# Where the second rows are turned in the first projection, and when two of its sums are made

## The chip, the cores and the metric

The kernel runs on one core of a Trainium2 chip. A core has TensorE (PE, matmuls from SBUF into PSUM), VectorE (DVE), ScalarE (ACT), GpSimd (POOL) and the DMA queues, of which SyncE (SP) issues most here. The engines run side by side, each through its own list of instructions, and wait for one another by semaphores. The metric is the device time of one execution in microseconds (us); several executions give a median.

## The reference, cut to what matters

One layer over 2048 rows of 1024 columns, all in float32: x_n = RMSNorm(x); an input projection z = x_n W_in; a pooling branch and a gated linear recurrence (HGRN2) on parts of z; sigmoid gates; an output projection; a gated feed-forward part; a last RMSNorm.

```python
xn = rmsnorm(x, norm1_g[l])
z = xn @ w_in[l]
u_pool, zq, zf, zi, zo, zg = jnp.split(z, splits, axis=-1)
```

The change touches the part of z that the kernel computes first: the columns of zi and zo (v and z in the kernel), 1024 columns in all, for the first 1024 rows.

## The kernel before, in words

**Blocks.** Rows are handled 1024 at a time (two halves of 512: `b0` and `b0 + 1`, "first rows" and "second rows"), so everything happens twice. A multiplication of the two row halves by the two halves of the weights is done in the seven-product way of Strassen and Winograd: seven passes P1 to P7 instead of eight. Each pass multiplies one form of the activations by one form of the weights.

**Forms.** `FORM` (line 52) names the activation form of each pass. B11 and B21 are the two column halves of the first rows, turned (transposed on TensorE by `transpose`, line 675, so that the columns lie on the partitions) and scaled by the norm's gain. B12 and B22 are the same of the second rows (B22 carried with a minus sign). The sums are T1 = B12 - B11, T2 = B22 - T1 (both by `minus`, line 762, straight from PSUM), T3 = B12 - B22 and T4 = B21 - T2. Each form has four tiles of 128 x 512, numbered 0 to 3. They are written T20 to T23, T30 to T33 and so on in the trace; x_t<-x_t,cols,... rows of L765 are the sums themselves.

**High and low halves.** A float32 product is made of three matmuls with operands cut to a shorter format. `split` (line 608) makes the two halves of a form: ScalarE casts the high half (x_T20h), then VectorE subtracts it from the whole and has the low half (x_T20l). The weights are cut the same way in `Stream.convert` (line 198): cast on ScalarE (L211), low half on VectorE (L212), into one of six operand tiles (`ops`), which come free when TensorE is done with them. A sum, its cast on ScalarE and its low half on VectorE are thus a round trip between two engines.

**The first projection**, `proj_io` (line 1166), runs the passes in the order of `IO_ORDER`: P1, P2, P6, P5, P7, P4, P3, which I call the first to the seventh pass. In each of them four weight tiles (k) are multiplied with four groups of 128 rows (j), each j with a PSUM bank of its own: 48 matmuls of 128 x 512 a pass. P1 goes into four banks called X, P2 into four Y, P6, P7 and P4 into the same four Z, P5 and P3 into four V. There are eight banks in all. `after` (line 1185) evacuates: after P6 it makes u2 = e1 - Z (L1191), after P7 u3 = Z - e1 (L1193), after P4 z from Z. Since P4 starts its banks Z anew, its first matmul follows u3. After P2 `out_v` (line 1174) makes v = e1 + Y and stores it from SP's queue.

**Weights of the passes.** P1, P2 and P4 take stored quarters of the weights. P6, P7 and P3 take sums of quarters, made in `plan_io`'s function `fn` (line 347, L351 on VectorE) when the tile's turn comes: two sums for each of P6's four tiles (w8 to w11 in the trace, for T20 to T23), one for P7's and P3's. Sums that are used again are stored to DRAM by `keep` and read back, among them P5's weights, which are P6's first sums.

**The second rows** are prepared by `forms_b_task` (line 746). When `go_io` is set, it does for k = 0 to 3: two banks of transpositions (`turned`), B22 on ScalarE, T1 and T2 on VectorE, T3 on VectorE, then the split of T2. After this loop come the splits of T1, of T3, then T4 and B22. The task is stepped once in so many matmuls (`mm`, line 145), or when a pass needs its form.

**What sets the order.** The kernel's text gives an order of issue, and a scheduler with a time model of its own then orders each engine's list when the program is built, by what depends on what. `behind(ins, other)` (line 239) binds an instruction to come after another on its engine, without a wait.

Of the kernel before, what the change touches and what calls it, by code (L numbers as in the profile page):

```python
# [15 lines left out]
ALU = mybir.AluOpType  # L16
# [36 lines left out]
FIRST = ("P1", "P6", "P5")  # L53
# [26 lines left out]
def tile_trunk(  # L80
# [26 lines left out]
    def slot(name, cols=TB, dt=F32):  # L107
        return slots.tile([P, cols], dt, tag="s", name=name, padded_shape=[P, 528])
# [4 lines left out]
    def f32(ap):  # L113
        return ap.bitcast(F32)
# [43 lines left out]
    class Stream:  # L158
# [39 lines left out]
        def convert(self):  # L198
            j = len(self.tiles)
            key, fn, raws = self.ops[j]  # L200
            while any(r.tile is None for r in raws):
                self.load()
            store_kept()
            v = fn(f"w{j}")
            t = opsp.tile([P, 2, 512], F32R, tag="ops", name=f"ops{j}")
            n = int(np.prod(v.shape[1:]))
            hi, lo = t[:, 0, :n], t[:, 1, :n]
            if len(v.shape) == 3:
                hi = hi.rearrange("p (a b) -> p a b", a=v.shape[1])
                lo = lo.rearrange("p (a b) -> p a b", a=v.shape[1])  # L210
            self.mark = act.copy(hi, v)  # L211
            low = dve.tensor_tensor(lo, v, f32(hi), ALU.subtract)  # L212
            if j in self.pins:
                for ins, other in zip((self.mark, low), self.pins[j]):
                    behind(ins, other)
            self.tiles.append((key, t))
            self.load_ahead()
# [21 lines left out]
    def behind(ins, other):  # L239

        tc.add_manual_dep(ins.ins, other.ins.name, mybir.DependencyInfo(
            mybir.DependencyClass.NoSync, mybir.DependencyReason.DATA), reason="behind")
# [17 lines left out]
    stream = Stream()  # L260
# [347 lines left out]
    def split(src, name, on_pool=False):  # L608
        hi = slot(name + "h", TB, F32R)
        lo = slot(name + "l", TB, F32R)  # L610
        if on_pool:
            pool.tensor_scalar(hi, src, 1.0, 0.0, ALU.mult, ALU.add)
        else:
            act.copy(hi, src)
        dve.tensor_tensor(lo, src, f32(hi), ALU.subtract)
        return hi, lo
# [10 lines left out]
    def n_step(ps, w, xk, j, first, last, mark=None, **kw):  # L627
        xh, xl = xk
        a, b = xh[:, j * P : (j + 1) * P], xl[:, j * P : (j + 1) * P]
        mm(ps, a, w[:, 0], start=first, stop=False, **kw)  # L630
        if mark is not None:
            behind(count[1], mark)
        mm(ps, a, w[:, 1], start=False, stop=False, **kw)
        mm(ps, b, w[:, 0], start=False, stop=last, **kw)
# [40 lines left out]
    def transpose(ps, xs, j, k):  # L675
        c = (k % 4) * P
        return pe.transpose(ps[:, j * P : (j + 1) * P], xs[j, k // 4][:, c : c + P], ident)
# [68 lines left out]
    def forms_b_task(src, gain, forms, full, after, go, early):  # L746
        name = f"{src[0]}{src[1]}_"
        xs = {}
        while early and not forms["B21"]:
            yield 1  # L750
        yield from norm_rows(src, name, xs, after, int(early))
        while not go():
            yield 2
        t1, b12, b22 = [], [], []

        def turned(k):
            ps = bank(f"{name}t{k}")
            for j in range(NT):
                transpose(ps, xs, j, k)
            return ps  # L760

        def minus(key, k, ps, x1, c=None, op=ALU.subtract):
            t = slot(f"{name}{key}{k}")
            c = gain + (k if c is None else c)
            dve.scalar_tensor_tensor(t, ps, col(c), x1, ALU.mult, op)  # L765
            return t


        t3 = []
        for k in range(4):  # L770
            while len(full["B11"]) <= k:
                yield 4
            p12 = turned(k)
            p22 = turned(k + 4)
            t = slot(f"{name}b{k}")
            act.activation(t, p22, AF.Copy, scale=negs[:, gain + k + 4 : gain + k + 5])
            b22.append(t)
            t1.append(minus("t1", k, p12, full["B11"][k]))
            t2 = minus("t2", k, p22, t1[k], k + 4)
            if src[0] == "m":  # L780
                t = slot(f"{name}t3{k}")
                pool.tensor_tensor(t, full["B11"][k], t2, ALU.subtract)
                t3.append(t)
            else:
                t3.append(minus("t3", k, p12, b22[k], op=ALU.add))
            forms["T2"].append(split(t2, f"{name}T2{k}"))
            full["T2"].append(t2)
            yield 1
        for k in range(4):
            forms["T1"].append(split(t1[k], f"{name}T1{k}"))  # L790
            yield 5
        for k in range(4):
            forms["T3"].append(split(t3[k], f"{name}T3{k}"))
            yield 1
        for k in range(4):
            while len(full["B21"]) <= k:
                yield 4
            t4 = slot(f"{name}t4{k}")
            (dve if src[0] == "x" else pool).tensor_tensor(t4, full["B21"][k], full["T2"][k],
                                                           ALU.subtract)  # L800
            forms["T4"].append(split(t4, f"{name}T4{k}"))
            forms["B22"].append(split(b22[k], f"{name}B22{k}"))
            yield 1
# [231 lines left out]
    def value(dst, a, ps):  # L1035
        if a is None:
            act.copy(dst, ps)
            return
        t, how = a
        if how == "from":  # L1040
            dve.tensor_tensor(dst, ps, t, ALU.subtract)  # L1041
        else:
            dve.tensor_tensor(dst, t, ps, ALU.add if how == "add" else ALU.subtract)  # L1043

    class Unit:
        def __init__(self, name, key, emit):
# [119 lines left out]
    def proj_io(b0, forms, late, vd, zd):  # L1166
        bk = {}
        e1, u2, u3 = {}, {}, {}

        def temp(d, key, j):  # L1170
            d[j] = slot(f"io{b0}_{key}_{j}")
            return d[j]

        def out_v(hf, j, a):
            t = slot(f"v{b0}_{hf}_{j}")
            value(t, a, bk["Y" if hf == 0 else "V"][j])
            sp.dma_start(vd[hf][:, j, :], t)

        def out_z(hf, j, a):
            t = slot(f"z{b0}_{hf}_{j}")  # L1180
            value(t, a, bk["Z" if hf == 0 else "V"][j])
            act.activation(t, t, AF.Silu)
            sp.dma_start(zd[hf][:, j, :], t)

        def after(p, j):
            if p == "P1":
                act.copy(temp(e1, "e1", j), bk["X"][j])
            elif p == "P2":
                out_v(0, j, (e1[j], "add"))
            elif p == "P6":  # L1190
                dve.tensor_tensor(temp(u2, "u2", j), e1[j], bk["Z"][j], ALU.subtract)  # L1191
            elif p == "P7":
                dve.tensor_tensor(temp(u3, "u3", j), bk["Z"][j], e1[j], ALU.subtract)  # L1193
                out_z(1, j, (u3[j], "add"))
            elif p == "P4":
                out_z(0, j, (e1[j], "from"))
            elif p == "P3":
                out_v(1, j, (u2[j], "sub"))

        for p in IO_ORDER:  # L1200
            if p == "P7" and not b0:
                setup.append(Task(setup_task()))
            xs = need(forms, FORM[p], late)
            kb = "Y" if p == "P2" else BANK[p]
            if kb not in bk:
                bk[kb] = [bank(f"io{b0}_{kb}_{j}") for j in range(NT)]
            for k in range(4):
                if (p, k) == GO_IO[b0 > 0]:
                    go_io[0] = True
                w = stream.get("io")  # L1210
                if (p, k, b0) == ("P1", 0, 0):
                    xh, xl = xs[0]
                    for n in range(3):
                        for j in range(NT):
                            mm(bk[kb][j], (xl if n == 2 else xh)[:, j * P : (j + 1) * P],
                               w[:, n % 2], start=n == 0, stop=False, skip_group_check=True)
                    stream.used(1)
                    continue
                for j in range(NT):
                    n_step(bk[kb][j], w, xs[k], j, p in FIRST + ("P2",) and k == 0, k == 3,  # L1220
                           skip_group_check=True)
                    if k == 3:
                        after(p, j)
                stream.used(1)
# [453 lines left out]
    for b in range(0, SEQ // TB, 2):  # L1678
        forms, task, late = nxt
# [55 lines left out]
```

## Time and profile before

| | us |
|---|---|
| median of 3 runs | 2563.47 |
| the three runs | 2560.06, 2567.12, 2563.47 |
| the profiled execution | 2558.88 |
| its span | 2557.1 |
| mean granted clock of TensorE in it | 0.996 |

The span runs from the first to the last instruction of the profiled execution; its time holds 1.8 us more around it. Rows of a timeline read: start, duration, engine, line, operation, tile written <- tiles read, shapes, and in brackets the idle time before it with the engine or DMA that ended it. A duration runs to the end of the last write, so two rows in sequence may overlap a little, and the pitch from start to start is what an instruction occupies. Tables of stretches give the busy time of each engine, then the granted clock (1.00 is full), the share of the DMA engines and GB/s. Line numbers are those of the kernel before; in the changed kernel, lines from 785 on stand some lines further down.

### The profile page before, as it was taken

Reading aid. Unit: us, or ns where it says so; the run is one execution under the profiler, and the core shown is the slowest. Engines: PE = TensorE matmul, PEld = TensorE weight load, DVE = VectorE, ACT = ScalarE, POOL = GpSimd, SP = SyncE. Lnnn points to the kernel's source line nnn. Section 1 sums busy time; section 2 is a strip of 40 time slices with the busy share of each in tenths; the row PEclk is TensorE's granted clock in tenths of the full one; section 3 lists DMA queues with packets and bytes.
Section 4 is the critical chain, followed back from the end, with each engine's and each line's share of the span. In section 5 each row is a group of like instructions: output and inputs, shape, how many; then the busy total and the mean of one; then the engine's idle time right before and its main releaser. Section 6 shows DMA issues by size and latency. Waiting matters only on the chain.

```text
span 2557.1 us, 35636 instructions
## 1 busy us (share of the span) xinstructions
PE 2518.8 (99%) x11508; PEld 2057.1 (80%) x11508; DVE 1980.0 (77%) x3518; ACT 1176.9 (46%) x2218; POOL 759.2 (30%) x1117
## 2 busy tenths in 40 slices
PE   8999999999999999999999999999999999999998
PEld 7787887888788888888887888888887888888887
DVE  7798778588899787885585877775978987778755
ACT  6433434324545454554454343442355554545534
POOL 1444344002544334461230111200034433325410
PEclk9999999999999999999999999999999999999999
DMA  7778758768788879997344343446442444446952
GB/s 249 246 195 220 211 179 243 235 209 245 193 244 245 222 227 240 258 356 257 131 153 149 98 137 111 129 155 224 147 162 95 155 150 144 147 138 230 332 163 99
DMA packets 252332, 493.76 MB, mean 193 GB/s; under 512 B 26544, under 2 KB 43056, under 8 KB 251824
## 3 DMA queue, kind: packets, MB, share of 16 engines
q1 hardware_dynamic: 185664, 315.70, 38.3%
q0 software_dynamic: 41504, 110.64, 16.8%
q10 hardware_dynamic: 24976, 65.13, 7.4%
q8 instruction: 91, 1.49, 0.2%
q14 instruction: 97, 0.79, 0.1%
HBM read 381.79 MB, written 187.17 MB: 222 GB/s over the span
## 4 chain that ended last, share of the span: by engine, by line
PE 92%; DVE 4%; issue 1%; DMA 1%; ACT 1%; POOL 0%; SPq 0%; ACTq 0%; DVEq 0%; POOLq 0%
PE dn_P L146 16%; PE up_Z L146 14%; PE up_X L146 10%; PE up_V L146 9%; PE wo_P L146 6%; PE gr_Z L146 4%; PE pb L146 3%; PE pa L146 3%; PE gr_X L146 3%; PE gr_V L146 3%; PE io_Z L146 2%; PE fr_Z L146 2%; PE io_V L146 2%; PE fr_X L146 2%; PE fr_V L146 2%; PE pl L918 1%
## 5 line engine op out<-in xcount | busy, mean ns | idle before, releaser
L211 ACT CAST ops<-raw 128x512 fp32r<-128x512 f32 x736 | 454.4, 620 | 844.4 <-PE dn_P L146 179.5
L212 DVE TENSOR_TENSOR ops<-raw,ops 128x512 fp32r<-128x512 f32 x736 | 547.5, 747 | 201.3 <-ACT ops L211 192.8
L1471 DVE SCALAR_TENSOR_TENSOR e<-h,cols,e 128x512 f32<-128x512 f32 x176 | 143.6, 818 | 31.2 <-ACT e L1469 24.1
L1469 ACT ACTIVATE e<-h,cols 128x512 f32<-128x512 f32 x176 | 142.5, 814 | 24.9 <-DVE h L1043 18.5
L1474 DVE SCALAR_TENSOR_TENSOR e<-h,cols,e 128x512 f32<-128x512 f32 x176 | 133.9, 769 | 2.8
L861 POOL DMA_DIRECT2D g_P<-dg_P x154 | 84.4, 555 | 162.4 <-PE dn_P L146 111.1
L1150 POOL TENSOR_TENSOR gf_P<-e,e 128x512 f32<-128x512 f32 x44 | 61.2, 1392 | 149.3 <-DVE e L1480 95.8
L1266 POOL TENSOR_TENSOR q<-q,qs 128x512 f32<-128x512 f32 x16 | 21.9, 1368 | 198.3 <-ACT qs L1265 150.8
L1150 POOL TENSOR_TENSOR gf_P<-gf_P,e 128x512 f32<-128x512 f32 x44 | 59.2, 1344 | 72.1 <-DVE e L1480 71.7
L1464 POOL COPY h<-h 128x2 f32<-128x2 f32 x88 | 40.2, 468 | 114.3 <-DVE h L1041 107.5
L1478 ACT ACTIVATE e<-e 128x512 f32<-128x512 f32 x88 | 55.6, 632 | 38.4 <-DVE e L1474 38.2
L1466 POOL COPY hist<-h 128x2 f32<-128x2 f32 x88 | 35.8, 407 | 118.7 <-DVE h L1043 116.9
L1043 DVE TENSOR_TENSOR h<-up_u,up_V 128x512 f32<-128x512 f32 x88 | 60.1, 683 | 13.4 <-PE up_V L146 12.9
L1303 ACT ACTIVATE gt<-gt,cols 128x512 f32<-128x512 f32 x48 | 34.8, 725 | 75.1 <-DVE gt L1043 61.0
L1125 DVE TENSOR_TENSOR x<-x,wo_P 128x512 f32<-128x512 f32 x88 | 56.1, 683 | 12.1 <-PE wo_P L146 11.9
L910 POOL COPY qm<-q 128x64 f32<-128x64 f32 x64 | 26.7, 438 | 114.7 <-DVE q L934 21.6
L1125 DVE TENSOR_TENSOR ac<-ac,dn_P 128x512 f32<-128x512 f32 x72 | 47.1, 682 | 16.5 <-PE dn_P L146 16.3
L918 PE MATMUL pl<-qm,k 128*128 128x192 f32 x256 | 48.3, 332 | 6.4 <-DVE qm L914 5.8
L1494 POOL DMA_DIRECT2D dg_P<-gf_P x88 | 50.7, 576 | 7.9 <-POOL gf_P L1150 7.2
L1077 ACT COPY up_e<-up_X 128x512 f32<-128x512 f32 x44 | 25.8, 586 | 57.9 <-PE up_X L146 50.7
L918 PEld LDWEIGHTS pl<-qm,k 128*128 128x128 f32 x256 | 43.5, 192 | 10.0 <-issue 4.3
L655 POOL TENSOR_SCALAR m_0ss<-m_0ss 128x1 f32<-128x1 f32 x4 | 0.9, 229 | 160.0 <-ACT m_xs L652 159.8
(1300 smaller groups left out, 8167.7 us busy)
## 6 DMA issues: line engine op xcount, KB each, us to landing
g_P<-dg_P POOLq DMA_DIRECT2D x154, 256.0 KB, 6.0
raw<-in_w_up_t SPq DMA_DIRECT2D x132, 256.0 KB, 3.1
raw<-in_w_in_t SPq DMA_DIRECT2D x98, 256.0 KB, 3.1
dg_P<-gf_P POOLq DMA_DIRECT2D x88, 256.0 KB, 3.8
dg_P<-e SPq DMA_DIRECT2D x66, 256.0 KB, 3.4
raw<-in_w_dn SPq DMA_DIRECT2D x66, 256.0 KB, 3.3
x<-in_x SPq DMA_DIRECT2D x64, 256.0 KB, 4.7
gd<-gt ACTq DMA_DIRECT2D x64, 256.0 KB, 3.1
```

Of the source, the lines that this page charges most:

```text
L146: count[1] = pe.matmul(*args, **kw)
L211: self.mark = act.copy(hi, v)
L212: low = dve.tensor_tensor(lo, v, f32(hi), ALU.subtract)
L861: eng.dma_start(t, d)
L918: pe.matmul(pa_[:, c * 192 : c * 192 + 192], ks[:, (i + c) * P : (i + c + 1) * P], mv[:, c].rearrange("p s x -> p (s x)"), start=True, sto ...
L1043: dve.tensor_tensor(dst, t, ps, ALU.add if how == "add" else ALU.subtract)
L1125: dve.tensor_tensor(t, t, ps[j], ALU.add if sg > 0 else ALU.subtract)
L1150: pin(eng.tensor_tensor(t, x0, x1, op))
L1469: in_turn(act.activation(t, h[:, 2:], AF.Identity, bias=col(o_cb + mt), scale=col(o_cw + 4 * MF + mt)))
L1471: in_turn(second(dve.scalar_tensor_tensor(t, h[:, 1 : 1 + TB], col(o_cw + 2 * MF + mt), t, ALU.mult, ALU.add)))
L1474: dve.scalar_tensor_tensor(t, h[:, 0:TB], col(o_cw + mt), t, ALU.mult, ALU.add)
L1478: in_turn(act.activation(g, g, AF.Silu))
```

## The change

It concerns the first 1024 rows' first projection alone (`early`, `not b0`).

- In the second pass, ahead of its second, third and fourth weight tile, the task of the second rows is stepped until one more unit k of T2 has been issued, and the first matmul of that weight tile (that of the first row group, bank Y 0) is bound to come after the unit's last transposition. Right after that, the weights are converted as far as the next tile of the third pass (tiles 9, 10 and 11, whose sums are w9 to w11).
- T3 is no longer made in that loop from B12's PSUM bank and B22 but later, in the loop that splits it, as B11 - T2, from SBUF.
- The four evacuations of v after the second pass are bound to come after the low half of the weight tile that was converted last.

```diff
-            low = dve.tensor_tensor(lo, v, f32(hi), ALU.subtract)
+            low = self.low = dve.tensor_tensor(lo, v, f32(hi), ALU.subtract)
...
-                transpose(ps, xs, j, k)
+                forms["turned"] = transpose(ps, xs, j, k)
...
-            else:
+            elif not early:
                 t3.append(minus("t3", k, p12, b22[k], op=ALU.add))
...
         for k in range(4):
+            if early:
+                t = slot(f"{name}t3{k}")
+                dve.tensor_tensor(t, full["B11"][k], full["T2"][k], ALU.subtract)
+                t3.append(t)
             forms["T3"].append(split(t3[k], f"{name}T3{k}"))
             yield 1
...
-            value(t, a, bk["Y" if hf == 0 else "V"][j])
+            ins = value(t, a, bk["Y" if hf == 0 else "V"][j])
+            if not (b0 or hf):
+                behind(ins, stream.low)
...
+                mark = None
+                if p == "P2" and k and not b0:
+                    while len(forms["T2"]) < k:
+                        late.step()
+                    mark = forms["turned"]
+                    while len(stream.tiles) < 9 + k:
+                        stream.convert()
                 w = stream.get("io")
...
-                    n_step(bk[kb][j], w, xs[k], j, p in FIRST + ("P2",) and k == 0, k == 3,
+                    n_step(bk[kb][j], w, xs[k], j, p in FIRST + ("P2",) and k == 0, k == 3, mark,
                            skip_group_check=True)
+                    mark = None
```

(`value` also returns its instruction now.)

More of the change, by code (lines that the diff above doesn't have):

```diff
@@ L1040, in value @@
         if how == "from":
-            dve.tensor_tensor(dst, ps, t, ALU.subtract)
-        else:
-            dve.tensor_tensor(dst, t, ps, ALU.add if how == "add" else ALU.subtract)
+            return dve.tensor_tensor(dst, ps, t, ALU.subtract)
+        return dve.tensor_tensor(dst, t, ps, ALU.add if how == "add" else ALU.subtract)
     class Unit:
```

## The prediction

> **What bounds the kernel now.** I read the page first, then the waits of TensorE, then a table of stretches of the first projection, then the rows around its two gaps. The page:
>
> ```profile
> span 2557.1 us, 35636 instructions
> PE 2518.8 (99%) x11508; PEld 2057.1 (80%) x11508; DVE 1980.0 (77%) x3518; ACT 1176.9 (46%) x2218; POOL 759.2 (30%) x1117
> ```
>
> TensorE is busy for 99% of the span, so an edit to the first projection matters by what TensorE loses there. Its waits (engine, line, for whom: total, times, longest) that belong to this stage:
>
> ```profile
> PE x_t L677 <- DVE x_t L765: 2.4, 2, 2.0
> PE io_Z L146 <- DVE x_t L765: 1.0, 1, 1.0
> PE io_Z L146 <- DVE io_u L1193: 0.6, 1, 0.6
> ```
>
> The first two are the change's target: transpositions of the second rows, and the third pass behind them, wait for PSUM banks that VectorE has not read yet. The third looks like a trifle. The stretches (length, busy time of PE, PEld, DVE, ACT, POOL, granted clock, DMA):
>
> ```profile
> 27.04:39.88 12.84, 12.84 (x66) 10.66 (x65) 10.23 (x19) 6.65 (x14) 1.81 (x5) 1.00 0.54 185
> 39.88:42.95 3.07, 1.03 (x10) 0.80 (x8) 2.93 (x6) 0.67 (x3) 0.00 (x0) 1.00 0.77 255
> 42.95:46.32 3.37, 2.06 (x8) 1.25 (x9) 3.27 (x6) 1.20 (x3) 0.00 (x0) 0.53 0.27 79
> 46.32:50.18 3.86, 3.86 (x9) 3.05 (x10) 3.79 (x6) 1.71 (x3) 0.00 (x0) 0.52 0.20 71
> 50.18:59.23 9.05, 9.05 (x40) 7.33 (x39) 8.56 (x15) 6.55 (x14) 0.00 (x0) 1.00 0.80 226
> 59.23:70.30 11.07, 11.07 (x49) 9.02 (x48) 11.07 (x20) 4.65 (x8) 4.73 (x2) 1.00 0.92 318
> 70.30:82.15 11.85, 11.28 (x49) 8.86 (x48) 10.22 (x18) 5.09 (x9) 8.29 (x12) 1.00 0.56 195
> 234.33:237.74 3.41, 2.98 (x8) 2.72 (x9) 3.41 (x14) 0.72 (x1) 0.59 (x2) 0.50 0.92 174
> ```
>
> Two things are to be seen. From 39.88 to 50.18 TensorE stands or runs at half clock. And from 39.88 to 82.15 VectorE is busy for all but 2.4 us (the differences of length and DVE column): it is the fuller engine here. TensorE's rows:
>
> ```profile
> 27.04 0.63 PE L146 MATMUL io_Y<-ops,x_f4h 128*128 128x512 f32 x2
> ...
> 36.06 1.91 PE L677 MATMUL x_t<-ident,x_xs 128*128 128x128 f32 x16
> ...
> 81.17 0.40 PE L146 MATMUL io_Z<-ops,x_T33l 128*128 128x512 f32 x1
> 82.15 0.70 PE L146 MATMUL io_Z<-ops,x_T40h 128*128 128x512 f32 x2 [0.58 <-DVE io_u L1193]
> ```
>
> The last two rows decide. The sixth pass (T4) writes the same four Z banks as the fifth (T3), so it cannot start before VectorE has read the first of them into u3. TensorE waited 0.58 us for that although it had already lost over 6 us. Without those losses it would have waited all the longer: the start of the sixth pass, 82.15, is VectorE's date. The question is what the change does to VectorE's way to u3.
>
> **The change, part by part, on VectorE and ScalarE.** Rows of before (start, duration, engine):
>
> ```profile
> 36.70 0.75 DVE L765 SCALAR_TENSOR_TENSOR x_t<-x_t,cols,x_b 128x512 f32<-128x512 f32 x1 [1.94 <-PE x_t L677]
> 37.91 0.75 DVE L765 SCALAR_TENSOR_TENSOR x_t<-x_t,cols,x_t 128x512 f32<-128x512 f32 x1 [0.46 <-ACT x_b L776]
> 38.58 0.74 DVE L765 SCALAR_TENSOR_TENSOR x_t<-x_t,cols,x_b 128x512 f32<-128x512 f32 x1
> 39.35 0.69 DVE L615 TENSOR_TENSOR x_T20l<-x_t,x_T20h 128x512 fp32r<-128x512 f32 x1
> ...
> 58.74 2.48 DVE L1191 TENSOR_TENSOR io_u<-io_e,io_Z 128x512 f32<-128x512 f32 x4 [0.38 <-PE io_Z L146]
> ...
> 73.91 0.72 DVE L212 TENSOR_TENSOR ops<-raw,ops 128x512 fp32r<-128x512 f32 x1 [0.65 <-ACT ops L211]
> ...
> 76.74 0.69 DVE L212 TENSOR_TENSOR ops<-raw,ops 128x512 fp32r<-128x512 f32 x1 [0.22 <-ACT ops L211]
> ...
> 78.70 0.68 DVE L799 TENSOR_TENSOR x_t<-x_b,x_t 128x512 f32<-128x512 f32 x1
> 80.11 0.69 DVE L615 TENSOR_TENSOR x_T43l<-x_t,x_T43h 128x512 fp32r<-128x512 f32 x1 [0.73 <-ACT x_T43h L614]
> ...
> 81.32 0.68 DVE L1193 TENSOR_TENSOR io_u<-io_Z,io_e 128x512 f32<-128x512 f32 x1
> ```
>
> ```profile
> 37.19 0.69 ACT L776 ACTIVATE x_b<-x_t,negs 128x512 f32<-128x512 f32 x1 [3.16 <-PE x_t L677]
> ...
> 73.25 0.63 ACT L211 CAST ops<-raw 128x512 fp32r<-128x512 f32 x1 [2.09 <-PE io_Z L146]
> ...
> 79.46 0.62 ACT L614 CAST x_T43h<-x_t 128x512 fp32r<-128x512 f32 x1 [1.71 <-issue]
> ```
>
> Two prices come out. A tensor-tensor of 512 columns occupies VectorE for 0.60 us (80.11 to 81.32 holds two). And a sum whose low half is the next instruction on VectorE costs it about 0.8 us of standing: the sum at 78.70, the high half on ScalarE at 79.46, the low half at 80.11, which is 1.41 us for 0.60 of work. The same trip lay between 37.91 and 39.35, but there t3 (38.58) filled the hole.
>
> The scheduler fixes each engine's order when the program is built, and the order of the changed one is known: between T20l and u3 VectorE has 67 instructions, where before it has 63. An instruction that waits holds up all behind it, as T43l does in the row at 80.11.
>
> *Turned earlier.* 35 matmuls now stand between 27.04 and the first transposition, where 39 took 9.02 us: 27.04 + 35 x 0.231 = 35.1 instead of 36.06. The first unit's four rows are interleaved with the second unit's, so t1 starts after eight transpositions of about 0.11, at 36.2; ScalarE's B22 reads the second bank from 36.45, t2 follows it at 37.2, and T20l comes at about 38.65. Gain **0.7 us**, which is only the date of the first unit. The next three units' transpositions no longer stand behind the second pass, but VectorE takes them up when it is through with the instructions ahead of them, and it had no hole there to fill (0.14 us between 39.88 and 42.95, 0.10 in the next 3.37). The pin costs TensorE nothing either: only the first bank's matmuls stay behind the transpositions, the other three banks' run ahead of them.
>
> *Weights behind, T3 away.* What stood before T20l and now follows it: two sums and the low half of the second T2 weight, and the first T3 (now B11 - T2): 4 x 0.60 = **+2.4**. The three other T3 change from 0.66 to 0.60 (by the 0.74 and 0.68 shown): **-0.2**. The shares of the output v evacuated behind the last T2 weight are as many as before, **0**; their banks are wanted only by the fourth pass, over 10 us of third pass away. Their store moves back on SP's queue past the last T2 sums' stores and four loads; those loads' weights are summed some 6 us later, so **0**. GpSimd's masks wait for a slot that T31's low half frees; they move with VectorE and are read by it behind u3 or just ahead, **0**. If one of these covers is gone, the price is the third rival's.
>
> *Bare round trips.* In the new order a low half directly follows its own sum at T22, at the fourth T2 weight, at T31, and at T40, T41 and T42 (T43 was bare already): before, t3 and casts of later weights stood in between. 6 x 0.8 = **+4.8**. The T4 and B22 group now stands whole behind T33, because T33's sum is made late, and ScalarE's T32 and T33 high halves stand behind weight casts that wait for operand buffers, as the 73.25 row did for the fifth pass's first tile. From both sides: 0 if something fills all six, 6 x 0.83 = 5.0 if none; I take 4.8, since the order names the next instruction.
>
> *Waits that go.* 0.38 (u2 waiting for a slowed TensorE), 0.65 and 0.22 (weight casts): -1.25; one weight's cast newly stands close on its sum, +0.2. **-1.0**; bounds -1.25 and 0.
>
> Sum on VectorE: -0.7 + 2.4 - 0.2 + 4.8 - 1.0 = **+5.3**. So u3 starts at 86.6 and the sixth pass at 87.5. TensorE is done with the fifth pass between 77.3 (T33l stands 13 instructions before u3, four of them bare round trips, and so starts near 75.4; four matmuls follow it) and 81.4 (as now), so it stands for 6 to 10 us with the whole program queued behind that one matmul.
>
> *Clock.* The 0.53 and 0.52 rows follow a wait of 2.04 us and last about 7 us; the 0.50 row at 234.33 lasts 3.4. At that clock nine matmuls took 3.86 us (46.32:50.18), 0.43 each for 0.231 before, so 46% of the slow time is lost. A wait of 6 us or more brings the slow clock too: 3.4 to 7 us of it, some of it spent waiting. Bounds 0 (clock kept) and 3.2; I take 4.5 x 0.46 = **+2.1**. The old slow stretch at 43 to 50 gives nothing back if it goes: it ended before VectorE's date.
>
> [...]
>
> *Afterwards.* From u3 on the order is the old one but for a few neighbours, and VectorE soon waits for TensorE, not the reverse:
>
> ```profile
> 118.32 0.69 DVE L1083 TENSOR_TENSOR fr_u<-fr_Z,fr_e 128x512 f32<-128x512 f32 x1 [6.18 <-PE fr_Z L146]
> ```
>
> So the delay is handed on whole. Sum: +5.3 + 2.1 = **+7.4 us**. The profiled execution took 2558.88 (span 2557.1 and 1.8 around it); it would become 2566.3. It lay 4.6 under the median shown, 2563.47; on the median the forecast is **2571 us**, +0.3%.
>
> **The rivals.**
> - *The gap closes and that is all* (faster). TensorE did 16 transpositions and 9 matmuls between 39.88 and 50.18, about 3.8 us of work in 10.3; the other 6.5 us go, and 2557 is left. It needs VectorE at u3 by 75 instead of 81.3. The bank waits speak for it, 11.07 busy of 11.07 against it. 5%.
> - *VectorE binds, but arrives as before* (not slower): the round trips are filled by other queued work or ScalarE answers sooner, so 4.8 shrinks to about nothing and the 0.7 and 1.0 pay for most of the 2.4. TensorE's wait at the sixth pass grows only by what it gained, without cost: 2563 to 2565. The point is whether a low half stands right behind its sum; 1.41 us at 78.70 speaks against it. 14%.
> - *More than that:* the T2 sums, made up to 6 us later, delay the copies that are stored and read back as the fourth pass's weights, or the slowed TensorE frees the operand buffer of the last fifth-pass casts late, so T33 slips as well; plus two full slow windows: +11 to +13, 2575. 14%.
>
> **How the numbers follow.** The forecast has 67%: 2571, on its own 2567 to 2574 (clock 0 to 3.2, waits 1 us). About 0.3%, 7.7 us, is what a measurement of this kernel tells from no change, and the forecast lies on that line: half of it counts as slower. Slower: 0.34 + 0.14 = 0.48. Within: 0.33 + 0.14 and the first rival, whose 6.5 us stay inside, mostly: 0.49. Faster: 0.03. The range 2563 to 2578 takes in the forecast, most of the second rival, the third, and runs that differ by 7 us; it leaves out the first.
>
> **What would show it.** Right: the first matmul on T40 waits 6 to 10 us for u3, near 87.5; low halves T22l, T31l, T40l to T42l each wait 0.7 to 0.8 for ScalarE; the clock is about 0.5 behind that wait; first transposition of second rows near 35.1. Wrong: T40 starts at 82 or earlier, or VectorE shows idle time ahead of u3 that TensorE ends. The whole forecast falls if VectorE's instructions of this stretch run shorter than 0.60.

## The result, and the profile after

| | before | after |
|---|---|---|
| median | 2561.11 us (10 runs, 2557.79 to 2567.12) | 2569.39 us (10 runs, 2565.36 to 2575.30) |
| ratio | 1 | 1.0033, 95% interval [1.0024, 1.0043] |
| the profiled execution | 2558.88 | 2567.91 |
| its span | 2557.1 | 2566.2 |
| first matmul on T40 | 82.15 | 89.53 |

The changed kernel is slower by 0.33% by the ratio, 8.3 us between the medians. Its page has as much work as before on TensorE and VectorE:

```profile
span 2566.2 us, 35634 instructions
...
PE 2517.7 (98%) x11508; PEld 2055.6 (80%) x11508; DVE 1980.7 (77%) x3518; ACT 1176.8 (46%) x2218; POOL 751.3 (29%) x1117
```

So the 9 us are waiting. TensorE's waits of this stage (total, times, longest), and its rows (start, duration):

```profile
PE io_Z L146 <- DVE io_u L1198: 8.4, 1, 8.4
...
PE io_Z L146 <- DVE x_t L765: 1.9, 2, 1.1
PE x_t L677 <- DVE x_t L765: 1.3, 2, 1.1
```

```profile
35.22 1.25 PE L677 MATMUL x_t<-ident,x_xs 128*128 128x128 f32 x10
...
44.45 0.70 PE L146 MATMUL io_Z<-ops,x_T20h 128*128 128x512 f32 x2 [0.77 <-DVE x_t L765]
...
80.04 1.09 PE L146 MATMUL io_Z<-ops,x_T33l 128*128 128x512 f32 x4
89.53 1.19 PE L146 MATMUL io_Z<-ops,x_T40h 128*128 128x512 f32 x2 [8.39 <-DVE io_u L1198]
```

The turning is earlier (35.22 for 36.06), the third pass too (44.45 for 46.32), and the clock stays at 1.00 there. TensorE's waits for the second rows' sums (x_t) are hardly shorter, 1.9 + 1.3 us for 2.4 + 1.0: what the early stretch gained is mainly the clock. Then all of it is lost in one wait: the fifth pass ends at 81.1, and the sixth starts 8.39 us later because VectorE makes its first u3 so late. Why it is late stands in VectorE's rows; these are all its waits of over 0.13 us from T20l to u3:

```profile
38.73 0.69 DVE L615 TENSOR_TENSOR x_T20l<-x_t,x_T20h 128x512 fp32r<-128x512 f32 x1 [0.69 <-ACT x_T20h L614]
...
45.85 0.69 DVE L615 TENSOR_TENSOR x_T22l<-x_t,x_T22h 128x512 fp32r<-128x512 f32 x1 [0.69 <-ACT x_T22h L614]
...
53.44 0.69 DVE L212 TENSOR_TENSOR ops<-w11s,ops 128x512 fp32r<-128x512 f32 x1 [0.74 <-ACT ops L211]
...
66.15 0.69 DVE L351 TENSOR_TENSOR w18s<-raw,raw 128x512 f32<-128x512 f32 x1 [1.82 <-DMA raw<-in_w_io]
...
71.14 0.69 DVE L615 TENSOR_TENSOR x_T31l<-x_t,x_T31h 128x512 fp32r<-128x512 f32 x1 [0.69 <-ACT x_T31h L614]
...
79.56 0.69 DVE L615 TENSOR_TENSOR x_T40l<-x_t,x_T40h 128x512 fp32r<-128x512 f32 x1 [0.69 <-ACT x_T40h L614]
...
82.14 0.69 DVE L615 TENSOR_TENSOR x_T41l<-x_t,x_T41h 128x512 fp32r<-128x512 f32 x1 [0.68 <-ACT x_T41h L614]
...
84.80 0.69 DVE L615 TENSOR_TENSOR x_T42l<-x_t,x_T42h 128x512 fp32r<-128x512 f32 x1 [0.68 <-ACT x_T42h L614]
...
87.48 0.69 DVE L615 TENSOR_TENSOR x_T43l<-x_t,x_T43h 128x512 fp32r<-128x512 f32 x1 [0.69 <-ACT x_T43h L614]
...
88.69 0.68 DVE L1198 TENSOR_TENSOR io_u<-io_Z,io_e 128x512 f32<-128x512 f32 x1
```

Eight of the nine are low halves that wait for their own cast on ScalarE. The ninth waits for a load: w18's sum, the third of the fifth pass's four weight sums (w16 to w19), each of two loaded parts. SP's queue shows why the load may be late; its rows (issue, time to issue them, how many) in the kernel before and in the changed one:

```profile
51.88 2.79 SPq L185 DMA_DIRECT2D raw<-in_w_io  x6
54.78 2.48 SPq L1177 DMA_DIRECT2D vd<-v  x3
```

```profile
54.45 1.85 SPq L185 DMA_DIRECT2D raw<-in_w_io  x4
56.39 2.19 SPq L1182 DMA_DIRECT2D vd<-v  x4
59.08 5.48 SPq L185 DMA_DIRECT2D raw<-in_w_io  x6
```

Before, six loads (the parts of w16, w17 and w18) went out ahead of three of v's four stores. Now four do, and w18's parts follow the stores, from 59.08 on. Experiment 11 tries whether that is the cause.

The stretch from T20l to u3 as a whole (length, then busy time of PE, PEld, DVE, ACT, POOL, clock, DMA), first in the kernel before, then in the changed one, with the slow clock behind the wait as a second row:

```profile
39.35:81.32 41.97, 38.62 (x164) 30.64 (x162) 39.57 (x64) 20.41 (x36) 12.87 (x12) 0.92 0.67 220
```

```profile
38.73:88.69 49.96, 38.12 (x167) 29.09 (x165) 42.48 (x68) 21.13 (x37) 5.24 (x12) 0.96 0.62 205
...
89.53:94.63 5.10, 5.10 (x12) 4.04 (x13) 5.07 (x11) 3.51 (x5) 2.01 (x10) 0.50 0.35 120
```

VectorE's date of u3 moved by 88.69 - 81.32 = 7.37 us: it started 0.62 earlier, was busy 2.91 longer (42.48 - 39.57) and idle 5.08 longer (7.48 - 2.40). Behind the wait, 12 matmuls took 5.10 us at half clock for 12 x 0.231 = 2.77 at full: 2.3 more.

### The profile page after: what moved, and what is told of

It reads as the page before. It is cut to its first block, busy times and chain, and to the rows that moved or that the text cites. A ratio compares the mean times of both kernels' runs of the same rounds, so it can differ in the third digit from the quotient of the medians.

```text
span 2566.2 us, 35634 instructions
## 1 busy us (share of the span) xinstructions
PE 2517.7 (98%) x11508; PEld 2055.6 (80%) x11508; DVE 1980.7 (77%) x3518; ACT 1176.8 (46%) x2218; POOL 751.3 (29%) x1117
## 4 chain that ended last, share of the span: by engine, by line
PE 72%; DVE 1%; ACT 0%; issue 0%; DMA 0%; POOL 0%; DVEq 0%; POOLq 0%
PE dn_P L146 16%; PE up_Z L146 14%; PE up_V L146 9%; PE up_X L146 9%; PE wo_P L146 3%; PE gr_Z L146 3%; PE gr_V L146 2%; PE pa L146 2%; PE pb L146 2%; PE gr_X L146 2%; PE io_Z L146 1%; PE fr_Z L146 1%; PE fr_X L146 1%; PE io_V L146 1%; PE fr_V L146 1%; PE pl L922 1%
## 5 line engine op out<-in xcount | busy, mean ns | idle before, releaser
L1477 POOL COPY h<-hist 128x2 f32<-128x2 f32 x88 | 46.2, 532 | 7.7 <-DVE m_T42l L615 7.7
```

Of the source, the lines that this page charges most:

```text
L1477: pool.tensor_copy(h[:, 0:2], hist[:, mt] if hf == 0 else hs[s, 0][:, TB : TB + 2])
```

## The experiments

All of them are edits of one of the two kernels, and only of the first rows' first projection. Their results together (T40 and its wait from each one's profile; the ratio to before with its interval):

| kernel | T40 at | waits | ratio |
|---|---|---|---|
| before | 82.15 | 0.58 | 1 |
| after | 89.53 | 8.39 | 1.0033 [1.0024, 1.0043] |
| 1 after, T3 in its old place | 85.96 | 4.88 | 1.0019 [1.0006, 1.0032] |
| 2 before, T3 late | 86.05 | 5.86 | 1.0013 [1.0004, 1.0021] |
| 3 after, v not bound | 88.82 | 8.74 | 1.0029 [1.0018, 1.0040] |
| 4 after, T3 in its old place, v not bound | 84.56 | 4.25 | 1.0033 [1.0021, 1.0045] |
| 12 the same again | 85.37 | 3.70 | 1.0023 [1.0011, 1.0035] |
| 5 after, wait filled with matmuls | 90.17 | 1.50 | 1.0021 [1.0012, 1.0031] |
| 6 before, u3 made ten times | 90.01 | 7.18 | 1.0033 [1.0017, 1.0048] |
| 7 after, T3 and T4 summed on GpSimd | 86.58 | none | 1.0024 [1.0014, 1.0033] |
| 8 before, the same | 84.60 | 0.79 | 1.0000 [0.9990, 1.0009] |
| 9 after, sums ahead of their splits | 86.75 | 5.24 | 1.0016 [1.0006, 1.0026] |
| 10 before, T3 late, sums ahead, B22 last | 83.32 | 1.87 | 1.0006 [0.9996, 1.0015] |
| 11 after, v stored later | 87.84 | 8.45 | 1.0024 [1.0015, 1.0032] |

A date in the span is good to some 0.8 us (rows 4 and 12 are one program). Ratios that overlap are not ranked; the dates and the waits carry the argument.

The theory: VectorE's date of u3 sets the sixth pass, and it is late by the round trips that stand bare in the new order. The rivals: the turning and its binding cost it; a load that comes late; VectorE is late by its amount of work; the slow clock has another cause.

### 1 and 2: T3's place alone

First, the changed kernel with T3 made in the loop again:

```diff
-            elif not early:
+            else:
                 t3.append(minus("t3", k, p12, b22[k], op=ALU.add))
...
-            if early:
-                t = slot(f"{name}t3{k}")
-                dve.tensor_tensor(t, full["B11"][k], full["T2"][k], ALU.subtract)
-                t3.append(t)
```

> The changed kernel with T3 made in its old place (from B12's bank and B22, right behind T2), all else as changed. Theory (bare round trips on VectorE): of the six new ones T22, T31, T40 and T41 have work between sum and low half again, so the first matmul on T40 starts 4 x 0.7 = 2.8 us earlier than in the changed kernel, at 86 to 87 instead of 89.5; the clock still falls behind that wait; time 2565 to 2567, ratio to before 1.0015 to 1.0025. Rival (the earlier turning and the order that it brings cost it, T3's place is neutral): T40 stays at 89.5 and the ratio at 1.0033.

Second, the kernel before with only that part of the change, that is, the same lines the other way round.

> The kernel before with only T3 moved (made late, as B11 - T2); no binding of the turning, no weights converted ahead, v free. Theory: T20, T22, T31, T41 and T42 become bare round trips, 5 x 0.7 = 3.5 us, less up to 1 us of waits that go: T40 at 84.6 to 85.7 instead of 82.15, ratio to before 1.001 to 1.002 (with some slow clock behind the wait). Rival (the turning costs it): T40 at 82 and the ratio 1.000. Second rival (T3's bank reading was what kept TensorE waiting): the early gap closes, T40 before 81, ratio under 1.

The sixth pass's first row in the first and in the second:

```profile
85.96 1.12 PE L146 MATMUL io_Z<-ops,x_T40h 128*128 128x512 f32 x2 [4.88 <-DVE io_u L1194]
```

```profile
86.05 1.19 PE L146 MATMUL io_Z<-ops,x_T40h 128*128 128x512 f32 x2 [5.86 <-DVE io_u L1196]
```

Undoing T3's move brings T40 3.6 us forward, and T22l, T31l, T40l and T41l no longer wait, the four that were named; the move alone puts 3.9 us onto before's T40 (0.35 us beyond the bounds given), though the third pass then starts 1.1 us earlier (45.24). In the second kernel T20l, T22l, T31l, T41l and T42l each wait 0.68 to 0.69 us for their casts, the five that were named. T3's late place is about half of the loss, and the rival that it is neutral falls. Reading B12's bank for T3 did hold TensorE up early, but freeing it earns nothing at T40.

### 3, 4 and 12: v's binding, and what the turning costs

```diff
             ins = value(t, a, bk["Y" if hf == 0 else "V"][j])
-            if not (b0 or hf):
-                behind(ins, stream.low)
```

> The changed kernel without the binding of v's evacuations. On VectorE they then stand between w11's sum and its low half, so that one round trip is filled; the stores of v still stand ahead of the loads of w18's parts on SP's queue. Theory: T40 0.7 us earlier than in the changed kernel, at 88.8; ratio to before 1.003. Rival (the binding is what costs, by the late load of w18's parts): the 1.82 us wait of w18's sum goes and T40 starts at 87 or earlier, ratio 1.002.

T40 starts at 88.82, as expected. w11's round trip is filled, but w18's sum waits the longer, so taking the binding away does not bring the load forward (v's stores still stand ahead of it):

```profile
65.61 0.69 DVE L351 TENSOR_TENSOR w18s<-raw,raw 128x512 f32<-128x512 f32 x1 [2.29 <-DMA raw<-in_w_io]
```

The fourth experiment takes both edits, T3 back and v unbound, and leaves the turning.

> The changed kernel with T3 in its old place and v unbound: what is left of the change is the turning's binding and the weights converted ahead. Theory: only T42's low half stands bare behind its sum more than before; T40 at 85 to 86, between before's 82.15 and the changed kernel's 89.5, the rest being two weight sums and a low half that moved behind T20l (1.8 us) and the load of w18's parts; ratio 1.001 to 1.002. Rival (turning alone is the loss): T40 at 88 or later. Rival (turning alone is a gain, spoiled by the rest): T40 at 81 or earlier, ratio under 1.

T40 started at 84.56, a little under what was expected, and the time was that of the whole change all the same, 1.0033. T40 2.4 us later does not explain a span 9.9 us longer (2567.0), so the same program was run once more, on another chip.

> The fourth experiment's kernel unchanged, for a second profile of one program. T40 should start at 84.6 within 0.7 again. If the slow stretches after 200 us come by chance (a fixed grid of 3.4 us windows that short waits of later stages happen to fill or not), they stand at other places than 239, 321, 683 and 1413; if they belong to the program, at the same places, and the ratio stays at 1.0033.

The second time it was 1.0023. The two profiles side by side, by stretches (length, TensorE's busy time, clock, DMA), the fourth experiment's first:

```profile
44.54:47.95 3.41, 2.66 (x11) 1.00 0.30 78
...
406.10:409.50 3.40, 3.40 (x20) 1.00 1.00 144
682.80:686.20 3.40, 3.40 (x10) 0.51 0.80 261
```

```profile
44.31:47.72 3.41, 2.84 (x7) 0.50 0.25 84
...
406.10:409.50 3.40, 3.40 (x16) 0.50 0.87 164
682.80:686.20 3.40, 1.91 (x8) 1.00 1.10 249
```

One program, and the slow stretches lie elsewhere, each one or two times 3.4 us long. A stretch of 3.4 us costs an estimated 3.4 x 0.46 = 1.6 us where TensorE is at work (by the 0.43 us for 0.231 that a matmul took in the slow stretch of before), so they alone can spread the runs of one kernel over several us. The slow stretches of the kernel before are of the same lengths (length, TensorE's busy time, clock, DMA):

```profile
43.18:50.01 6.83, 5.51 (x17) 0.50 0.24 78
234.33:237.74 3.41, 2.98 (x8) 0.50 0.92 174
316.25:319.66 3.41, 3.41 (x11) 0.50 0.98 352
```

They start 191.15 and 81.92 us apart, 56.06 and 24.02 times 3.41; the changed kernel's, at 84.40 and 244.82, 160.42 us apart, 47.04 times 3.41. So by these three differences they lie on a grid of some 3.41 us within one execution, as the twelfth expectation supposed; that waits decide which of its places run slow is shown at two places alone, by experiment 5 and by the first rows of the two fences above. (The profiles of experiments 4 and 12 are of two chips, but on one chip, too, the mean granted clock of the twelfth's ten runs goes from 0.993 to 0.997.)

The first rows of the fences of experiments 4 and 12 show how little decides. In both profiles TensorE has waited 1.98 and 0.6 us just before, for the same sums. In the 3.41 us that end where these rows begin (in the first counted back from its slow stretch at 85.5 in steps of 3.41) it was busy for 2.01 us in the first and for 1.66 in the second; the clock stayed in the first and fell in the second.

The turning alone costs 2.4 to 3.2 us at T40; how much more than that it costs in the time is not settled by 1.0033 and 1.0023. In these two profiles w18's sum still waits for its load, 2.18 and 2.53 us, as v's stores still stand ahead of it. That is most of what the turning costs at T40; the turning with the stores moved back was not tried by itself.

### 5: the clock by itself

```diff
+                    if (p, k, j, b0) == ("P7", 3, 3, 0):
+                        for n in range(30):
+                            ins = pe.matmul(bk["V"][3], zeros, xs[3][0], start=False,
+                                            stop=n == 29, skip_group_check=True)
+                            behind(ins, count[1])
...
```

> The changed kernel with 30 matmuls of a zero weight tile put behind the fifth pass; they add nothing to the V bank that they write and keep TensorE at work for 30 x 0.231 = 6.9 us of its 8.4 us wait for u3. Theory (what stands behind the wait is a slow clock that comes from the standing): the first matmul on T40 still starts at 89.5, the clock stays at 1.00 from 84 to 95, and the 2.3 us lost there go: ratio to before 1.0024 instead of 1.0033. Rival (the clock falls for another reason, or the 2.3 us have another cause): the slow stretch at 84 to 95 stays, and so does the ratio.

`zeros` is a tile of zeros, and the sixth pass's first matmul is bound to come after the last of the 30. The rows, then the stretch of the slow clock in the changed kernel and in this one:

```profile
81.51 7.16 PE L1242 MATMUL io_V<-x_T33h,zeros 128*128 128x512 f32 x30
90.17 0.70 PE L146 MATMUL io_Z<-ops,x_T40h 128*128 128x512 f32 x2 [1.50 <-DVE io_u L1201]
```

```profile
84.40:94.63 10.23, 5.11 (x12) 4.07 (x13) 9.07 (x18) 5.54 (x9) 3.02 (x14) 0.50 0.17 60
```

```profile
84.40:94.63 10.23, 8.73 (x38) 6.78 (x37) 8.78 (x18) 5.35 (x8) 2.66 (x12) 1.00 0.11 38
```

T40 stays where it was (the whole profile lies 0.7 us later), TensorE is at work, and the clock stays at 1.00. The mean granted clock says the same over all runs: 0.9956 in the changed kernel's ten, 0.9972 in this one's eleven, which is 0.0016 x 2567 / 0.5 = 8 us less of slow clock (a slow stretch grants 0.5). So the slow clock came from standing. By the rows it costs 2.3 us on top of the wait; the ratio goes from 1.0033 to 1.0021, 3 us, but these intervals overlap.

### 6: the wait made on purpose in the kernel before

```diff
-                dve.tensor_tensor(temp(u3, "u3", j), bk["Z"][j], e1[j], ALU.subtract)
+                temp(u3, "u3", j)
+                for n in range(10 if (b0, j) == (0, 0) else 1):
+                    dve.tensor_tensor(u3[j], bk["Z"][j], e1[j], ALU.subtract)
```

> The kernel before with its first u3 made ten times instead of once: 9 x 0.60 = 5.4 us more on VectorE right ahead of the sixth pass, nothing else. Theory (the sixth pass starts on VectorE's date and the delay is handed on whole): T40 starts at 82.15 + 5.4 = 87.5 with a wait of some 6 us, the slow clock follows it (1 to 2.3 us), ratio to before 1.0025 to 1.003. Rival (TensorE has slack there or makes it up later): T40 at 84 or earlier, or the ratio under 1.001.

```profile
82.58 1.41 DVE L1195 TENSOR_TENSOR io_u<-io_Z,io_e 128x512 f32<-128x512 f32 x2
84.10 5.76 DVE L1195 TENSOR_TENSOR io_u<-io_Z,io_e 128x512 f32<-128x512 f32 x8
```

The ten take 0.72 us each, not 0.60, so the nine added ones make 6.5 us, and VectorE was at the first of them at 82.58 instead of 81.32 in this profile (its T20l lies 0.63 us later, and the first u2 waits 0.63 us longer for TensorE, neither by the edit); T40 starts at 90.01, 7.9 us later, and the ratio is 1.0033. A kernel with before's whole order and only VectorE's date spoiled behaves as the changed one does: the date sets the sixth pass, and TensorE makes nothing up.

### 7 and 8: the sums on GpSimd

In both kernels T3 and T4 are summed on GpSimd right behind T2, T3 as B11 - T2:

```diff
-            if src[0] == "m":
+            if src[0] == "m" or early:
                 t = slot(f"{name}t3{k}")
                 pool.tensor_tensor(t, full["B11"][k], t2, ALU.subtract)
...
+            if early:
+                t = slot(f"{name}t4{k}")
+                pool.tensor_tensor(t, full["B21"][k], t2, ALU.subtract)
```

> The changed kernel with the sums T3 and T4 made on GpSimd as soon as their T2 is there, T3 as B11 - T2 and T4 as B21 - T2, 8 instructions. Theory: VectorE loses 8 x 0.60 = 4.8 us of work and the round trips of T31, T40, T41, T42 and T43 (5 x 0.7 = 3.5): u3 at 88.7 - 8.3 = 80.4, T40 at 81 to 82.5 with a wait under 3 us and little or no slow clock, ratio to before 0.9995 to 1.0010. Rival (GpSimd's sums come late or slow VectorE down): T40 at 84 or later, ratio over 1.0015.

> The same in the kernel before: T3 and T4 summed on GpSimd, the turning and the weights in the old order. Theory: VectorE loses 8 sums (4.9 us) and T43's round trip and is at u3 by 76, so TensorE sets the sixth pass's start: the first T3s no longer stand between VectorE and the bank of the next unit, the third pass starts near 45 and T40 at 78.5 to 80.5 instead of 82.15; ratio to before 0.9985 to 0.9995. Rival (the gap at 40 to 50 is VectorE's other work, and the gain is lost in waits of the passes in between): T40 at 82, ratio 1.000.

Both expectations failed: T40 at 86.58 and 84.60, ratios 1.0024 and 1.0000. In the seventh the rival had it; in the eighth the ratio is the rival's, with T40 later than either said. GpSimd's and VectorE's rows of the seventh:

```profile
38.46 1.30 POOL L782 TENSOR_TENSOR x_t<-x_b,x_t 128x512 f32<-128x512 f32 x1 [8.42 <-DVE x_t L765]
39.72 1.71 POOL L790 TENSOR_TENSOR x_t<-x_b,x_t 128x512 f32<-128x512 f32 x1
```

```profile
39.06 1.24 DVE L615 TENSOR_TENSOR x_T20l<-x_t,x_T20h 128x512 fp32r<-128x512 f32 x1 [0.69 <-ACT x_T20h L614]
40.23 1.76 DVE L351 TENSOR_TENSOR w9s<-raw,raw 128x512 f32<-128x512 f32 x1
42.02 0.69 DVE L351 TENSOR_TENSOR w9s<-w9s,raw 128x512 f32<-128x512 f32 x1
```

While GpSimd sums, these two VectorE instructions take 1.24 and 1.76 us; when GpSimd is through, the next takes 0.69. The 0.6 us that a sum took off VectorE it paid back in the early stretch, where the third pass waits for it: it starts at 47.32 here and at 48.04 in the eighth. That the sums beside them are what lengthens VectorE's instructions is read from these rows; it was not tried by itself. In the eighth VectorE then waits 1.28 and 0.34 us for masks of GpSimd's, of which more below.

### 9: the order alone

The T3 sums stand together ahead of the T3 splits, and likewise T4's; no instruction is added or taken away:

```diff
-        for k in range(4):
-            if early:
+        if early:
+            for k in range(4):
                 t = slot(f"{name}t3{k}")
...
+            if early and not k:
+                while len(full["B21"]) < 4:
+                    yield 4
+                for i in range(4):
+                    t4_of(i)
```

> The changed kernel with the four T3 sums made one behind the other ahead of their splits, and the four T4 sums likewise: the same instructions on the same engines in another order, so that at T31, T40, T41, T42 and T43 other sums or low halves stand between a sum and its low half. Theory: five round trips of 0.7 us go, T40 at 89.5 - 3.5 = 86.0, some slow clock stays; ratio to before 1.0015 to 1.0025. Rival (VectorE is late by its amount of work, not by its order): T40 at 89 or later, ratio 1.0033.

T40 came at 86.75 for 86.0, and the ratio was 1.0016, between the expected bounds. The low halves of T40 to T43 wait for nothing now. A new wait stands behind them:

```profile
83.25 0.68 DVE L615 TENSOR_TENSOR x_T43l<-x_t,x_T43h 128x512 fp32r<-128x512 f32 x1
85.21 0.20 DVE L590 CAST m<-mf 128x64 uint8<-128x64 f32 x1 [1.28 <-POOL mf L585]
```

Five trips of 0.69 us went, 3.4, and a mask that GpSimd makes for a later stage took 1.3 back; why it is late is told below. That VectorE is late by its amount of work alone is out: the amount is the same here.

### 10: a version meant to beat both

The kernel before with T3 late, the sums ahead as in the ninth, and B22's splits in a loop behind T4's.

> The kernel before with T3 made late (as in the second experiment), the T3 and T4 sums ahead of their splits, and B22's splits behind T4's: no binding of the turning, no GpSimd. From the second experiment's T40 at 86.05: 4 round trips x 0.7 (T31, T41, T42, T43) and two low halves of B22 (1.2) that now follow u3 go, so T40 at 82.0 with a wait of 2 us at most, and no slow clock behind it: ratio to before 0.9985 to 0.9995, the first version below both. Rival (what the early stretch gains is not TensorE's to keep): T40 at 82 as before, ratio 0.9998 to 1.0005; a second (T3 late costs in any order): T40 at 84 or later.

```profile
79.15 0.20 DVE L590 CAST m<-mf 128x64 uint8<-128x64 f32 x1 [1.28 <-POOL mf L585]
80.91 0.20 DVE L590 CAST m<-mf 128x64 uint8<-128x64 f32 x1 [0.33 <-POOL mf L585]
82.38 0.20 DVE L590 CAST m<-mf 128x64 uint8<-128x64 f32 x1 [0.67 <-POOL mf L585]
```

It missed: T40 at 83.32 and 1.0006, not told apart from before. Waits for three masks take 2.3 us ahead of u3 (at 82.48). No version here beat the kernel before.

### 11: the load of w18's parts

The stores of v are kept back and issued at the fifth pass's start, bound behind the last load by then:

```diff
-            sp.dma_start(r.tile, src)
+            self.loaded = sp.dma_start(r.tile, src)
...
-            sp.dma_start(vd[hf][:, j, :], t)
+            if b0 or hf:
+                sp.dma_start(vd[hf][:, j, :], t)
+            else:
+                held.append((vd[hf][:, j, :], t))
...
+                if p == "P5" and not k:
+                    for args in held:
+                        behind(sp.dma_start(*args), stream.loaded)
```

> The changed kernel with the four stores of v moved on SP's queue behind the two loads of w18's parts and the two after them; VectorE's order is that of the changed kernel. Theory (w18's sum waits 1.82 us because its loads stand behind v's stores on SP's queue): the loads are issued by 57.8 instead of 59.1, the wait falls to 0.5 us or less, and T40 starts at 88 instead of 89.5. Rival (the loads are late because their buffers or the DMA engines are): the wait stays over 1.3 us and T40 at 89.

w18's sum no longer waits, in a kernel whose VectorE order is that of the changed one, and T40 comes at 87.84, 1.7 us earlier:

```profile
64.33 0.68 DVE L351 TENSOR_TENSOR w18s<-raw,raw 128x512 f32<-128x512 f32 x1
```

The stores' place on SP's queue was the cause of that wait.

## Why the prediction was right, and where it was not

The forecast was 2571, +0.3%; measured +0.33%, 2569.39. By its steps:

- **What bounds.** Right. The sixth pass's start is VectorE's date (experiment 6), and TensorE's early gain, 1.9 us and the slow clock at 43 to 50, was waited away. The fifth pass ended at 81.1, inside the 77.3 to 81.4 given. One thing in the description is wrong: the sixth pass does not start its banks Z anew, it adds to them. Its first matmul has to follow u3 either way, since u3 must read the bank first.
- **Turned earlier.** First transposition 35.22 (35.1 forecast), T20l 38.73 (38.65): -0.62 for -0.7.
- **Weights behind, T3 away.** +2.2 as forecast, counted from start to start as the prediction counts. The busy time grew by 2.9, because the instruction ahead of a wait shows its whole 0.69 us, where one in an unbroken row adds 0.60, and there are more waits.
- **Bare round trips.** All six stand where they were named, with 0.68 to 0.74 us of idle time each. Counted from start to start less 0.60 (0.67 at T22), they make 0.76 to 0.84 each and 4.7 for 4.8. Experiments 1, 2 and 9 move T40 as they come and go.
- **Waits that go.** All three did, 1.25 of idle time, 1.5 from start to start. Four short new ones, for casts, take 0.7 back where 0.2 was given: -0.8 for -1.0.
- **The step that failed:** the move of v's stores on SP's queue was priced "**0**". The prediction looked at the four loads that the stores move past, whose weights "are summed some 6 us later"; those were in time. It overlooked the next two, w18's parts, which had stood ahead of three of the stores and now stand behind all four. w18's sum waited 1.82 us, 1.9 from start to start, and experiment 11 takes that wait away. With it the sum at u3 is -0.6 + 2.2 + 4.7 + 1.9 - 0.8 = +7.4, the 7.37 measured, for +5.3.
- **Clock.** 2.3 for 2.1, by another route: 10.2 us slow instead of 4.5, but half of that was spent standing. The slow stretch at 244.82 below is 3.41 us long; the one here, 84.40 to 94.63, is three times that.
- **Afterwards.** 7.4 + 2.3 = 9.7 at the sixth pass, 9.1 at the span's end. Part of that difference is the later slow stretches: before's profile has two, at 234 and 316, after's one, at 245. In the changed kernel:

```profile
244.82:248.23 3.41, 3.24 (x9) 0.50 0.71 202
316.25:319.66 3.41, 3.41 (x26) 1.00 0.55 153
```

  That is an estimated 1.6 us; about 1 us the other way was not traced.
- **The time.** That it came out near 2571 is luck in part. The date was missed by 2 us, and the forecast stood on the median of three runs, 2563.47, which ten runs put at 2561.11; the two errors cancel.

The rivals: the first did not come. The early gap closed in part (the slow clock went, the waits stayed at 3.2 us for 3.4), and nothing of it reached the sixth pass, as VectorE was at u3 by 88.7 and not by 75. That the round trips would be filled was wrong for every one of them. The third was there in part: a late load, and three lengths of 3.41 us at the slow clock for its "two full slow windows".

## What to carry to other kernels

Before an edit that feeds TensorE earlier, find the next point where it waits for another engine, and ask whether that engine gets there earlier too; otherwise the gain only makes that wait longer, and a long one brings the slow clock (10.2 us of it here, with a wait of 8.39). On an in-order engine a producer's step and the step that needs another engine's answer to it want other work between them: here 0.7 us for each pair. Stores that come to stand ahead of loads on a queue delay them (1.82 us at the loads' reader here), so look at every load whose place against them changes, and price it by when it lands, not by when it is used.

## What was not expected of the hardware

VectorE without holes seems to shut GpSimd out. The same GpSimd instruction on a mask of 128 x 64, in after, before and experiment 9:

```profile
72.18 0.77 POOL L583 TENSOR_SCALAR_AFFINE_SELECT mf<-mf 128x64 f32<-128x64 f32 x1
```

```profile
65.72 8.06 POOL L583 TENSOR_SCALAR_AFFINE_SELECT mf<-mf 128x64 f32<-128x64 f32 x1
```

```profile
72.78 11.68 POOL L583 TENSOR_SCALAR_AFFINE_SELECT mf<-mf 128x64 f32<-128x64 f32 x1
```

Spans on GpSimd are rough, but the two long ones end where VectorE stands: in before at 73.8, inside the 0.65 us that VectorE waits until 73.91; in experiment 9 at 84.5, inside the 1.28 us until 85.21, a wait for this very mask. In experiment 10 it took 12.27 us and ended at 78.4, inside VectorE's wait of 1.28 us until 79.15; experiment 8 has a wait of the same 1.28 us, until 80.34. Up to there VectorE issued one instruction each 0.60 us. In the changed kernel, whose VectorE has holes all along, it took 0.77. So filling the holes (8, 9 and 10) made the mask the next wait. That is read from where the spans end, and was not tried by itself.

The clock fell not only after long waits: in the kernel before it fell at 43.18, after one of 2.04 us, for 6.83 us, twice 3.41. Experiments 4 and 12 show that the same waits, 1.98 and 0.6 us, can keep it or lose it: 1.00 in the one, 0.50 in the other.
